# Index scores of a decoder trunk: the rectified scores of two neighbouring pieces in one tile, added by one VectorE operation

## The chip, the cores and the metric

One core of one Trainium2 chip runs the whole program. The metric is the device time of one execution in microseconds (us), and the time of the kernel before is the median of three runs. Times inside the program come from one profiled execution, counted from the start of its span. The engines are PE (TensorE), DVE (VectorE), ACT (ScalarE), POOL (GpSimd) and SP (SyncE, which issues most DMAs); each has its own queue and works it off in order.

## The reference

Two post-norm layers run over 2048 tokens of width 1024: forgetting attention, then sparse attention (DSA) with a light indexer. The change lies in the indexer of the second layer. For each token it computes eight heads of scores against all earlier tokens, rectifies them, weighs them by a number per token and head, sums over the heads, and keeps the 256 largest:

```python
isc = jnp.einsum('bqhd,bsd->bqhs', qi_b, ki).astype(jnp.float32) * di ** -0.5
isc = jnp.einsum('bqhs,bqh->bqs', jax.nn.relu(isc), wi_b)
isc = jnp.where(kpos[None, None, :] <= qpos[None, :, None], isc, -jnp.inf)
_, idx = lax.top_k(isc, k_sel)
```

The selected keys then go through an ordinary softmax attention, a SiLU gate and an output projection.

## The kernel before

The program runs in phases. After the first layer's attention and output projection comes the stage around the change: the projections of the second layer (`dsa_jobs`: `first`, `second`, `rest`), with the indexer's jobs woven in between them by `weave`. Then the second layer's attention and its output projection follow. The build uses a scheduler (`TCA`, "schedule_with_timeline_sim") that plays the program through with modelled times and so fixes the order of every engine's queue; the order of jobs in the source gives the priorities.

The index works on 14 query tiles of 128 tokens, tiles 2 to 15, in three groups (`GROUPS`): 7 to 2, 11 to 8, 15 to 12. Scores of query tile `qt` span n = (qt + 1) * 128 keys and stand in SBUF as one row of f32 per token (`x`, in the tiles GA, GB, GC: the first group in GA, the second in GB, the third in GC for tiles 15 and 14 and in GA again for 13 and 12). While one group is scored, the threshold search of the group before it runs (`step`, `move`, `finish`: counting passes on ACT, L1554, and on DVE, L1550, and chains of small operations on DVE).

`scores` (L1464) makes one query tile. It loads the queries `qs` (L1470, tag QS, two buffers), and for every head cuts the n keys into pieces of at most 512 columns (`cuts`, L1094): 1 piece for tiles 2 and 3, 2 for tiles 4 to 7, 3 for 8 to 11 (of which the last has 256 to 512 columns), 4 for 12 to 15. A piece is

- two matmuls (L1477, L1478) into a PSUM bank that `unit` gives out in a cycle of S, U, S, U, S (three banks S, two U),
- one ACT operation (L1480): scale and Relu from PSUM into an SBUF tile of tag SC (three buffers of 512 f32),
- one DVE operation: for head 0 a multiplication by the token's weight into `x` (L1483, TENSOR_SCALAR), for heads 1 to 7 a multiplication and addition onto `x` (L1485, SCALAR_TENSOR_TENSOR).

The projections of the same stage use the banks T and O, evacuated by ACT and DVE (L371, L378, L379) or, where a rotation is applied, by `rope` (L1247 to L1250); its table `kcs` is loaded into an SC buffer. Weights of a projection come from DRAM to RW (L353), are scaled and split by ACT and POOL (L341, L328, L325). Tag QS is a buffer of 1024 f32 and also serves, before this stage, a layer-norm row, and after it the first masks of the second attention (L964, read by L1054).

Each phase lays its tiles out in the order of `ORDER` with the sizes (in f16 elements) of `SIZE`; phase 6, the index, lies behind the eight KV tiles that hold the projections' input.

Of the kernel before, what the change touches and what calls it, by code (L numbers as in the profile page):

```python
# [15 lines left out]
F16 = mybir.dt.float16  # L16
OP = mybir.AluOpType
AF = mybir.ActivationFunctionType
# [29 lines left out]
BUFS = {"W": 6, "E": 8, "RW": 3, "QS": 2, "SC": 3, "ty": 9, "tz": 4, "tb": 2, "mb": 2}  # L48
PHASE = ({"KV": 8}, {"K": 4, "V": 2, "PT": 1, "PU": 1, "PX": 1, "PR": 4, "PP": 3, "I": 1, "N": 3},
         {"K": 4, "V": 2, "PT": 1, "PU": 1, "PX": 1, "PR": 4, "PP": 3, "M": 1, "N": 3}, {"P": 8},  # L50
         {"A": 3, "X": 15}, {"P": 8}, {})
ORDER = ((), ("N", "I", "PR", "PT", "pad1", "PU", "K", "PP", "V", "PX"),
         ("N", "M", "PX", "PR", "K", "V", "PP", "pad2", "PT", "PU"), ("pad3", "P"), ("A", "X"), (),
         ("st", "GB", "u", "GA", "GC", "spare"))
SIZE = {"K": 2048, "V": 4096, "PT": 8192, "PU": 8192, "PX": 8192, "PR": 4096, "PP": 4096, "I": 128, "N": 256,
        "M": 2432, "pad1": 3200, "pad2": 896, "pad3": 4096, "P": 4096, "A": 4096, "X": 4096, "st": 4096,
        "u": 3584, "spare": 4096, "GA": 8448, "GB": 10752, "GC": 7936}
TURNED = ("PT", "PU", "PX")

PS_BUFS = {"S": 3, "T": 2, "U": 2, "O": 1}  # L60
# [170 lines left out]
class Trunk:  # L231
# [1232 lines left out]
    def scores(self, qt, st, x):  # L1464
        nc = self.nc
        n = (qt + 1) * 128
        self.stack(n)
        qs = self.t("QS", [128, 8, 128], F16)
        ready = nc.gpsimd.memset(x[:, n - 1:n], 0.0)
        load = nc.sync.dma_start(qs, self.scr["qis"].rearrange("(h p) t -> p h t", p=128)  # L1470
                                 [:, :, qt * 128:(qt + 1) * 128])
        self.follow(load, ready, "no scores without a place for them")
        for h in range(H):
            for a, b in self.cuts(n):
                w = b - a
                ps = self.unit()
                nc.tensor.matmul(ps[:, :w], qs[:, h], st[:, 0, a:b], start=True, stop=False)  # L1477
                nc.tensor.matmul(ps[:, :w], qs[:, h], st[:, 1, a:b], start=False, stop=True)  # L1478
                t = self.t("SC", [128, w])
                nc.scalar.activation(t, ps[:, :w], AF.Relu, scale=self.scales[:, 24:25])  # L1480
                w1 = self.wi[:, qt, h:h + 1]
                if h == 0:
                    nc.vector.tensor_scalar(x[:, a:b], t, w1, None, op0=OP.mult)  # L1483
                else:
                    nc.vector.scalar_tensor_tensor(x[:, a:b], t, w1, x[:, a:b], op0=OP.mult, op1=OP.add)  # L1485

    def select(self, tiles, st):
        nc, V = self.nc, self.nc.vector
# [185 lines left out]
```

## Time and profile before

| | us |
|---|---|
| median of three runs (2772.9 to 2783.97) | 2780.16 |
| the profiled execution | 2781.16 |
| its span | 2779.4 |
| first and last start of the score additions (L1485) | 1451.2, 1862.0 |
| last projection matmul ahead of the second attention | 2055.17 |

The profile gives for each engine its busy time in any stretch, for each group of instructions the count, the mean duration and the idle time of its engine just ahead of them with what ended that idle time, and for each wait who waited for whom. "Busy" of PE overlaps from one matmul to the next. The granted clock is TensorE's, as a share of the full 2.4 GHz.

### The profile page before, as it was taken

Reading aid. Unit: us, or ns where it says so; the run is one execution under the profiler, and the core shown is the slowest. Engines: PE = TensorE matmul, PEld = TensorE weight load, DVE = VectorE, ACT = ScalarE, POOL = GpSimd, SP = SyncE. Lnnn points to the kernel's source line nnn. Section 1 sums busy time; section 2 is a strip of 40 time slices with the busy share of each in tenths; the row PEclk is TensorE's granted clock in tenths of the full one; section 3 lists DMA queues with packets and bytes.
Section 4 is the critical chain, followed back from the end, with each engine's and each line's share of the span. In section 5 each row is a group of like instructions: output and inputs, shape, how many; then the busy total and the mean of one; then the engine's idle time right before and its main releaser. Section 6 shows DMA issues by size and latency. Waiting matters only on the chain. (4 is left out here: it accounts for less than half of the span.)

```text
span 2779.4 us, 44011 instructions
## 1 busy us (share of the span) xinstructions
PE 2517.8 (91%) x15919; PEld 1636.5 (59%) x15919; DVE 1888.0 (68%) x4662; ACT 1419.7 (51%) x2283; POOL 858.8 (31%) x601
## 2 busy tenths in 40 slices
PE   8788989999988889889999989899978888888898
PEld 7688534444665666668845444444435666666687
DVE  4786655444766666667748899888955666666565
ACT  6464343322665666632326876774535666666310
POOL 3465643330333334442210211110013333333421
PEclk9899999999999999999999999999989999999999
DMA  7456645214988888864332432222678888777642
GB/s 263 162 187 204 211 126 173 76 65 151 210 204 171 184 188 181 165 198 141 124 97 61 123 90 64 69 75 82 197 217 190 192 178 184 173 163 151 183 144 88
DMA packets 583809, 424.20 MB, mean 153 GB/s; under 512 B 398048, under 2 KB 473584, under 8 KB 583584
## 3 DMA queue, kind: packets, MB, share of 16 engines
q1 hardware_dynamic: 580544, 412.78, 56.2%
q10 hardware_dynamic: 1984, 4.20, 0.5%
q0 software_dynamic: 1056, 4.36, 0.4%
q8 instruction: 125, 2.05, 0.3%
q14 instruction: 100, 0.82, 0.1%
HBM read 219.88 MB, written 109.08 MB: 118 GB/s over the span
## 5 line engine op out<-in xcount | busy, mean ns | idle before, releaser
L325 POOL TENSOR_TENSOR PP<-PR,PP 128x640 f16<-128x640 f32 (+3 forms) x192 | 375.8, 1971 | 697.0 <-ACT PP L1076 525.5
L1068 ACT ACTIVATE PR<-PR,ty,small 128x1152 f32<-128x1152 f32 (+15 forms) x256 | 330.1, 1290 | 249.5 <-DVE ty L1067 245.5
L325 POOL TENSOR_TENSOR W<-RW,W 128x512 fp32r<-128x512 f32 (+1 forms) x124 | 160.0, 1310 | 540.7 <-ACT W L328 469.5
L325 POOL TENSOR_TENSOR W<-A,W 128x512 f16<-128x512 f32 x114 | 136.5, 1218 | 228.8 <-ACT W L328 192.2
L320 PEld LDWEIGHTS <-W 128*128 128x128 f16 x1184 | 116.3, 98 | 147.1 <-issue 13.9
L321 PEld LDWEIGHTS <-W 128*128 128x128 f16 x1184 | 116.3, 98 | 137.9 <-issue 2.9
L319 PEld LDWEIGHTS <-W 128*128 128x128 f16 x1184 | 116.6, 98 | 137.3 <-issue 3.2
L1076 ACT ACTIVATE PP<-PR 128x640 f16<-128x640 f32 (+3 forms) x192 | 186.2, 980 | 18.0 <-DMA PX<-PP 7.5
L320 PEld LDWEIGHTS <-V 128*128 128x128 f16 x1152 | 117.0, 102 | 104.4 <-issue 81.8
L319 PE MATMUL T<-KV,W 128*128 128x512 f16 x464 | 176.9, 381 | 0.4 <-DVE E L1250 0.4
L320 PE MATMUL T<-KV,W 128*128 128x512 f16 x464 | 177.1, 382 | 0.0
L321 PE MATMUL T<-KV,W 128*128 128x512 f16 x464 | 176.9, 381 | 0.0
L328 ACT ACTIVATE W<-RW 128x512 fp32r<-128x512 f32 (+1 forms) x124 | 73.4, 629 | 181.6 <-PE U L320 93.6
L1054 DVE CUSTOM_DVE_ANT_0 PR<-S,W,ty 128x512 f32<-128x512 f32 (+3 forms) x209 | 138.8, 664 | 38.0 <-PE S L1049 18.1
L319 PEld LDWEIGHTS <-V 128*128 128x128 f16 x1152 | 116.9, 101 | 64.0 <-DMA PX<-PP 17.0
L319 PE MATMUL S<-K,E 128*128 128x512 f16 (+3 forms) x379 | 132.3, 349 | 11.5 <-DVE ty L1054 10.7
L378 ACT ACTIVATE SC<-E,tz 128x512 f16<-128x512 f32 (+1 forms) x78 | 50.8, 682 | 172.5 <-DVE E L540 102.6
L320 PE MATMUL S<-K,E 128*128 128x512 f16 (+3 forms) x379 | 132.3, 349 | 0.0
L321 PE MATMUL S<-K,E 128*128 128x512 f16 (+3 forms) x379 | 131.9, 348 | 0.0
L1480 ACT ACTIVATE SC<-S,small 128x512 f32<-128x512 f32 (+2 forms) x182 | 111.8, 635 | 35.4 <-DVE GC L1485 7.1
L321 PEld LDWEIGHTS <-V 128*128 128x128 f16 x1152 | 117.2, 102 | 20.1 <-issue 0.8
L1088 PE MATMUL T<-ident,PR 128*128 128x128 f32 x768 | 116.6, 277 | 3.4 <-DVE PU L325 1.7
(503 smaller groups left out, 7836.0 us busy)
## 6 DMA issues: line engine op xcount, KB each, us to landing
A<-in_fw SPq DMA_DIRECT2D x38, 512.0 KB
QS<-in_fw SPq DMA_DIRECT2D x32, 512.0 KB
E<-scr_g SPq DMA_DIRECT2D x64, 256.0 KB
scr_og<-SC SPq DMA_DIRECT2D x64, 256.0 KB
RW<-scr_og SPq DMA_DIRECT2D x64, 256.0 KB
E<-scr_q SPq DMA_DIRECT2D x62, 256.0 KB
V<-scr_v SPq DMA_DIRECT2D x28, 512.0 KB
scr_g<-E SPq DMA_DIRECT2D x48, 256.0 KB
```

What stands on the lines that cost most here:

```text
L319: first = mm(o, lh, rh, start=start, stop=False, skip_group_check=True)
L320: mm(o, lh, rl, start=False, stop=False, skip_group_check=True)
L321: mm(o, ll, rh, start=False, stop=stop, skip_group_check=True)
L325: eng.tensor_tensor(out=o, in0=a, in1=b, op=OP.subtract)
L328: self.nc.scalar.activation(hi, src, AF.Copy)
L378: nc.scalar.activation(out[0], src, AF.Copy, scale=scale)
L1054: nc.vector.tensor_tensor_reduce(out=row[:, lo:hi], in0=sc[:, lo - a:hi - a], in1=bias, op0=OP.add, op1=OP.min, scale=-1.0, scalar=3e38 if ...
L1068: nc.scalar.activation(row, row, AF.Exp, bias=up, scale=neg, accum_out=cs["l"][:, j:j + 1])
L1076: nc.scalar.activation(hi, row, AF.Copy)
L1088: nc.tensor.transpose(ps[:, (k - a) * 128:(k - a + 1) * 128], row[:, k * 128:(k + 1) * 128], self.ident)
L1480: nc.scalar.activation(t, ps[:, :w], AF.Relu, scale=self.scales[:, 24:25])
```

## The change

The queries move to a tag of their own, `qs`, with two buffers at the end of phase 6. The score pieces move from SC to QS: two neighbouring pieces of one head, or the single last one, are rectified by their ACT operations into one QS tile side by side, and one DVE operation multiplies, or multiplies and adds, over both, up to 1024 columns. Matmuls, ACT operations, PSUM banks and loads keep their number and size.

```diff
-         {"A": 3, "X": 15}, {"P": 8}, {})
+         {"A": 3, "X": 15}, {"P": 8}, {"qs": 2})
...
-         ("st", "GB", "u", "GA", "GC", "spare"))
+         ("st", "GB", "u", "GA", "GC", "spare", "qs"))
...
-        "u": 3584, "spare": 4096, "GA": 8448, "GB": 10752, "GC": 7936}
+        "u": 3584, "qs": 1024, "spare": 4096, "GA": 8448, "GB": 10752, "GC": 7936}
...
-        qs = self.t("QS", [128, 8, 128], F16)
+        qs = self.t("qs", [128, 8, 128], F16)
...
         for h in range(H):
-            for a, b in self.cuts(n):
-                w = b - a
-                ps = self.unit()
-                nc.tensor.matmul(ps[:, :w], qs[:, h], st[:, 0, a:b], start=True, stop=False)
-                nc.tensor.matmul(ps[:, :w], qs[:, h], st[:, 1, a:b], start=False, stop=True)
-                t = self.t("SC", [128, w])
-                nc.scalar.activation(t, ps[:, :w], AF.Relu, scale=self.scales[:, 24:25])
+            cuts = self.cuts(n)
+            for i in range(0, len(cuts), 2):
+                two = cuts[i:i + 2]
+                lo, hi = two[0][0], two[-1][1]
+                t = self.t("QS", [128, hi - lo])
+                for a, b in two:
+                    ps = self.unit()[:, :b - a]
+                    nc.tensor.matmul(ps, qs[:, h], st[:, 0, a:b], start=True, stop=False)
+                    nc.tensor.matmul(ps, qs[:, h], st[:, 1, a:b], start=False, stop=True)
+                    nc.scalar.activation(t[:, a - lo:b - lo], ps, AF.Relu, scale=self.scales[:, 24:25])
                 w1 = self.wi[:, qt, h:h + 1]
                 if h == 0:
-                    nc.vector.tensor_scalar(x[:, a:b], t, w1, None, op0=OP.mult)
+                    nc.vector.tensor_scalar(x[:, lo:hi], t, w1, None, op0=OP.mult)
                 else:
-                    nc.vector.scalar_tensor_tensor(x[:, a:b], t, w1, x[:, a:b], op0=OP.mult, op1=OP.add)
+                    nc.vector.scalar_tensor_tensor(x[:, lo:hi], t, w1, x[:, lo:hi], op0=OP.mult, op1=OP.add)
```

## Rows read from the trace of the kernel before

**Rows 1.** The page, part 1: busy time of each engine, its share of the span and its instructions.

```profile
PE 2517.8 (91%) x15919; PEld 1636.5 (59%) x15919; DVE 1888.0 (68%) x4662; ACT 1419.7 (51%) x2283; POOL 858.8 (31%) x601
```

**Rows 2.** Busy time by stretch: the stretch and its length; busy time (and instructions) of PE, PE's weight loads, DVE, ACT and POOL; PE's granted clock; the share of the DMA engines and GB/s.

```profile
1448.00:1533.00 85.00, 83.04 (x428) 42.22 (x426) 66.57 (x132) 56.89 (x104) 7.08 (x6) 1.00 0.22 59
1533.00:1600.00 67.00, 62.78 (x288) 29.29 (x288) 59.01 (x167) 55.96 (x107) 15.87 (x13) 0.95 0.43 124
1600.00:1863.00 263.00, 238.63 (x1111) 108.97 (x1109) 244.96 (x768) 197.63 (x357) 36.48 (x34) 0.99 0.28 75
1863.00:2055.00 192.00, 188.38 (x866) 84.83 (x865) 163.46 (x375) 93.59 (x136) 10.97 (x14) 0.99 0.46 149
...
1533.00:1545.00 12.00, 7.78 (x23) 3.07 (x23) 10.37 (x24) 9.33 (x16) 1.97 (x2) 0.72 0.32 92
```

**Rows 3.** PE's waits from 1448 to 1863 us (who waited, for whom: us in total, times, longest), and below them the same wait of L1477 from 1600 to 1863 us alone (us, times).

```profile
PE S L1477 <- ACT SC L1480: 19.0, 19, 3.1
PE U L1477 <- ACT SC L1480: 9.8, 10, 2.9
...
  ACT SC L1480: 24.2, 24
```

**Rows 4.** ACT's waits from 1600 to 1863 us.

```profile
ACT RW L341 <- DMA RW<-in_dw: 14.8, 8, 3.8
ACT SC L1480 <- DVE GC L1485: 9.9, 5, 3.8
ACT SC L1480 <- DVE GB L1485: 9.7, 10, 1.9
...
ACT SC L1480 <- DVE GA L1485: 4.6, 7, 1.8
```

**Rows 5.** The chain that ended last, where the projections end: start, length, what.

```profile
2037.25 0.22 PE O L319
2055.17 0.23 PE O L321
```

**Rows 6.** The instructions of L1480 and of L1485: engine, operation, out<-in, count, duration in ns as least, median and most, first and last start, and their shapes.

```profile
L1480 ACT ACTIVATE SC<-S,small x182: 461/678/757, 1449.9 to 1860.2; 128x512 f32<-128x512 f32 x118, 128x384 f32<-128x384 f32 x35, 128x256 f32<-128x256 f32 x29
L1480 ACT ACTIVATE SC<-U,small x122: 454/682/742, 1449.3 to 1858.0; 128x512 f32<-128x512 f32 x82, 128x384 f32<-128x384 f32 x21, 128x256 f32<-128x256 f32 x19
...
L1485 DVE SCALAR_TENSOR_TENSOR GA<-SC,flog,GA x126: 466/740/1717, 1451.2 to 1862.0; 128x512 f32<-128x512 f32 x70, 128x384 f32<-128x384 f32 x28, 128x256 f32<-128x256 f32 x28
L1485 DVE SCALAR_TENSOR_TENSOR GB<-SC,flog,GB x84: 474/744/1724, 1538.9 to 1688.1; 128x512 f32<-128x512 f32 x56, 128x384 f32<-128x384 f32 x14, 128x256 f32<-128x256 f32 x14
...
L1485 DVE SCALAR_TENSOR_TENSOR GC<-SC,flog,GC x56: 569/737/1350, 1694.7 to 1781.0; 128x512 f32<-128x512 f32 x49, 128x384 f32<-128x384 f32 x7
```

**Rows 7.** Prices of DVE operations. First two of the timeline (start, length, count at the end, idle time ahead), then groups by shape from 1448 to 1863 us (busy us, mean ns of one, idle ahead).

```profile
1455.27 3.40 DVE L1485 SCALAR_TENSOR_TENSOR GA<-SC,flog,GA 128x512 f32<-128x512 f32 x5 [2.02 <-ACT SC L1480]
...
1466.06 0.75 DVE L1485 SCALAR_TENSOR_TENSOR GA<-SC,flog,GA 128x512 f32<-128x512 f32 x1 [0.92 <-ACT SC L1480]
...
L1609 DVE SCALAR_TENSOR_TENSOR spare<-GA,sv,small 128x1024 bf16<-128x1024 f32 x1 | 1.3, 1283 | 0.0
...
L1483 DVE TENSOR_SCALAR GA<-SC,flog 128x512 f32<-128x512 f32 x10 | 4.7, 479 | 0.7 <-ACT SC L1480 0.7
...
L1483 DVE TENSOR_SCALAR GA<-SC,flog 128x256 f32<-128x256 f32 x4 | 1.4, 346 | 0.0
```

**Rows 8.** The instructions of L1485 from 1600 to 1863 us, columns as in rows 6; those of GC stand there.

```profile
L1485 DVE SCALAR_TENSOR_TENSOR GB<-SC,flog,GB x56: 474/739/1656, 1601.4 to 1688.1; 128x512 f32<-128x512 f32 x30, 128x256 f32<-128x256 f32 x14, 128x384 f32<-128x384 f32 x12
...
L1485 DVE SCALAR_TENSOR_TENSOR GA<-SC,flog,GA x56: 466/741/752, 1788.5 to 1862.0; 128x512 f32<-128x512 f32 x35, 128x256 f32<-128x256 f32 x14, 128x384 f32<-128x384 f32 x7
```

**Rows 9.** Three small operations of the search on DVE, from the timeline. The second doesn't read what the first wrote; the third reads what the second wrote.

```profile
1924.63 0.16 DVE L1574 SCALAR_TENSOR_TENSOR sv<-sv 128x4 f32<-128x4 f32 x1
1924.71 0.16 DVE L1575 SCALAR_TENSOR_TENSOR sv<-sv 128x4 f32<-128x4 f32 x1
1924.90 0.17 DVE L1503 TENSOR_TENSOR sv<-sv 128x8 f32<-128x8 f32 x1
```

**Rows 10.** The timeline around 1535 us; in brackets the idle time ahead and what ended it.

```profile
1534.29 0.74 DVE L1247 SCALAR_TENSOR_TENSOR SC<-O,small,SC 64x512 f32<-64x512 f32 x1
...
1536.41 0.69 ACT L1480 ACTIVATE SC<-U,small 128x512 f32<-128x512 f32 x1 [2.12 <-DVE GB L1483]
...
1537.15 0.40 PE L1477 MATMUL U<-st,QS 128*128 128x512 f16 x1 [2.93 <-ACT SC L1480]
```

**Rows 11.** Three rows of SP's timeline, and the first reads of a mask in QS (L1054, as in rows 6).

```profile
1816.86 1.28 SPq L964 DMA_DIRECT2D QS<-scr_mask  x3
...
1848.52 1.46 SPq L353 DMA_DIRECT2D RW<-in_dw  x2
...
1856.64 2.33 SPq L964 DMA_DIRECT2D QS<-scr_mask  x2
...
L1054 DVE CUSTOM_DVE_ANT_0 PR<-U,QS x2: 672/677/682, 2049.3 to 2059.2; 128x512 f32<-128x512 f32 x2
```

**Rows 12.** A wait of ACT for weights, and PE's wait behind it, from their timelines.

```profile
1786.52 1.35 ACT L341 ACTIVATE RW<-RW,small 128x512 f32<-128x512 f32 x2 [3.77 <-DMA RW<-in_dw]
...
1788.49 0.38 PE L1477 MATMUL S<-st,QS 128*128 128x512 f16 x1 [3.07 <-ACT SC L1480]
```

## The prediction

> **What bounds the kernel now.** I read the page's busy shares first [rows 1]: PE is busy for 91% of the span, DVE for 68%, so nothing of DVE is worth time unless it holds PE up somewhere. The edited lines run between 1448 and 1863 us, so next comes the table of stretches [rows 2]. It shows three regimes. From 1448 to 1533 PE is busy for 83.0 of 85 us and DVE idles for 18 us: PE bounds. From 1533 to 1600 one stretch of 12 us stands out: PE 7.8 of 12 us busy, granted clock 0.72. From 1600 to 1863 the roles are mixed: DVE is busy for 245.0 of 263 us and PE for 238.6, so PE loses 24.4 us. From 1863 on PE is full again (188.4 of 192).
>
> The waits say what PE lacked. In the whole stage nearly all of it is one row pair: matmuls of L1477 that wait for a PSUM bank, which ScalarE (L1480) has not emptied yet: 19.0 + 9.8 us, of which 24.2 us lie between 1600 and 1863 [rows 3]. ScalarE in turn waited there for VectorE's score operations, 9.9 + 9.7 + 4.6 us, because no place was free for the rectified piece, and apart from that 14.8 us for weights from DRAM [rows 4]. So the chain is DVE (L1485) -> SC place -> ACT -> PSUM -> PE. After it PE works to 2055 us, where the last projection leaves and attention begins [rows 5]. What PE gains between 1448 and 1863 moves that point, and everything behind it, one for one.
>
> **The change part by part.**
>
> *Merged operations.* The stage has 182 + 122 = 304 pieces, so 304 ACT operations, 126 + 84 + 56 = 266 additions (L1485), and therefore 38 multiplications (L1483) [rows 6]. By `cuts`, query tiles 2 and 3 have one piece per head, 4 to 7 two, 8 to 11 three, 12 to 15 four. Pairing saves 1 operation per head for tiles 4 to 11 and 2 for tiles 12 to 15: 16 per head, 128 in all; 176 DVE operations are left. ACT and PE keep all theirs.
>
> The price of a merge: five additions of 512 columns in a row take 3.40 us, one alone 0.75, so each further one costs (3.40 - 0.75)/4 = 0.66 us; there is an overlap of 0.09 us with its neighbour. The kernel before has no addition of 1024 columns with these tiles, but the same operation on 1024 columns takes 1.283 us at L1609 [rows 7]; less the same overlap that is 1.19. A merge thus saves 2 x 0.66 - 1.19 = 0.13 us of DVE time. Upper bound: without any overlap 2 x 0.744 (the median in [rows 6]) - 1.28 = 0.21; the multiplications give the same (2 x 0.346 - 0.479 = 0.21, [rows 7]). Lower bound: none, since it is the count of starts that falls; a saving below zero would need a 1024-column operation above 1.33 us, which no row shows. I take 0.13, because DVE runs back to back where it matters.
> The Trainium skill ("Perfetto Trace Analysis", Optimizing Scalar/DVE Operations) puts VectorE's overhead per instruction on SBUF at about 60 ns and says that grouping into larger operations improves throughput if the engine is saturated. By that figure the sum below would be 64 x 0.06 = 3.8 us and the time an estimated 2776; the rows show about twice the figure.
>
> *Where it counts.* The 32 merges of tiles 4 to 7 fall before 1533, where DVE idles for 18 us: nothing. Should that cover be gone, they would be worth 4 us. The third group (15, 14) and the first buffer's second use (13, 12) lie wholly between 1600 and 1863 [rows 6, 8]: 64 merges, 64 x 0.13 = 8.3 us. Of the second group (11 to 8, tile GB) 56 of 84 additions lie there [rows 8], so 32 x 56/84 = 21 merges or 2.8 us; I count none of it, because of the next part.
>
> *Places.* Three SC places of 512 columns become two QS places of up to 1024. Tiles 12 to 15 need two pairs per head: each place takes a pair, the lead grows from three pieces to four. Tiles 4 to 7 the same. Tiles 8 to 11 need a pair and a single piece, so the pairs always fall into one place and the singles into the other. ACT can then refill the pair's place only after VectorE has read it. Back to back, a head took 2 x 0.66 + 0.5 = 1.9 us on DVE; now fill (2 x 0.68, the median of L1480 in [rows 6], about 1.3 with the overlap of two in a row) and read (1.2) come one after the other: 2.5 us. That is up to 0.65 us per head for 32 heads, 21 us, if nothing stands between the heads on DVE. These 32 heads are spread over 150 us, 4.7 us each, with other work of DVE between them, so most of it should be covered. I set it against the 2.8 us above and keep 21 us as the bound of the range.
>
> *Repeated sums.* With one operation per head in tiles 4 to 7, an addition reads what the one directly ahead of it wrote. Small operations of the search start 0.08 us apart when the second doesn't need the first, and 0.19 when it does [rows 9]. 32 x 0.11 = 4 us, all before 1533, hidden by DVE's idle 18 us; 4 us if not.
>
> *Places shared no longer.* SC is left to the `kcs` table and others. Around 1534 the table held one of three SC places while VectorE was turning it; ACT waited 2.12 us, PE 2.93 us, and the clock fell to 0.72 [rows 2, 10]. Now three score pieces' worth of room stays. That stretch of 12 us lost 4.2 us of PE and 12 x 0.28 = 3.4 us of clock: 0 to 7.6 us, of which I take 0, since DVE itself was busy for most of it.
>
> *Queues.* The loads of `qs` have the same count, size and number of places (two), only another address, behind `spare`, where no tile lay before in this phase: 0. The loads of attention's masks go to QS places as well: three at 1817 us, two at 1857 [rows 11]. They now need VectorE to have read the scores, so they come at 1862 at the earliest, 190 us ahead of their first reader at 2049 [rows 11]: 0. But if the planner leaves the first of them in SP's queue at 1817, the weight loads at 1848 stand behind it for up to 14 us. ACT's waits for such loads already put PE back by 3.07 us at 1788 [rows 12]; a repeat would cost about that.
>
> **The sum.** The profiled execution took 2781.2 us (span 2779.4), 1.0 above the median of 2780.2; the change is a difference, so it is taken from the median: 2780.2 - 8.3 = 2772 us.
>
> **The rivals.**
> (1) *All of the score waits go.* PE's 24.2 us between 1600 and 1863, less what began as a late weight load (3.07 at 1788, [rows 12], and perhaps as much again), and the 7.6 us around 1534: 18 + 8 = 26 us, 2754. For it: ACT's waits on score operations sum to 24 us [rows 4], and a backlog shrinks faster than the load. Against: DVE stays over 90% busy there.
> (2) *The waits are a matter of order.* The queues are ordered by a planner that plays the program through; what PE meets is a mismatch of its times with the real ones, and DVE's 8 us become idle time between search steps. 2780.
> (3) *The single place of the pairs decides.* Tiles 8 to 11 run at 2.5 instead of 1.9 us per head, from 1535 to 1688; it decides as soon as VectorE has less than 0.65 us of other work between two heads, and PE's lead of five PSUM banks (two matmuls of 0.22 us each, [rows 5], so 2.2 us) is used up, as it was at each of the waits in [rows 3]. 32 x 0.65 = 21 us, 2801; the same with half of it, 2790. For it: the group's additions are among those that ACT waits for most [rows 4]. Against: 4.7 us per head.
> The rule of the Trainium skill that speaks for this one stands in the same section of "Perfetto Trace Analysis": where VectorE isn't saturated but causes bubbles on other engines, "breaking up instructions may allow work to be completed sooner". By that rule, the trace agrees that DVE's score operations cause PE's bubbles; with 93% busy it is near saturation, so both halves of the section apply in part.
> (4) *It doesn't do what it says*: the wide operation costs as much as two. the operation at L1609 speaks against it; 2780, told with (2).
>
> **How the numbers follow.** A measurement of this kernel can tell about 0.5% from no change: 13.9 us. Forecast, a gain of 4 to 14 us: 0.33. Rival (1) and all gains above 14 us: 0.30. Rivals (2) and (4), within 4 us: 0.12. A part of (3), a loss of 4 to 14 us: 0.05. Rival (3) in full: 0.20. So faster by over 0.5%: 0.30; within 0.5%: 0.33 + 0.12 + 0.05 = 0.50; slower: 0.20. The range runs from a little below rival (1) to half-way and a bit into rival (3): 2750 to 2796.
>
> **What would show it.** Right: 176 operations on L1483 and L1485, wide ones at about 1.28 us; busy DVE time of L1483 and L1485 down by some 27 us; PE's wait for L1480 between 1600 and 1863 down from 24 to about 16 us; PE's last projection some 8 us earlier than 2055. Wrong: ACT waiting longer for the second group's places (GB) than the 9.7 us of before, or PE's waits moving to other lines; mask loads with SP waiting behind them for tens of us. The forecast fails if DVE's saved time reappears as idle time while PE's waits stay.

## The result

| | before | after |
|---|---|---|
| median of nine runs, us | 2775.59 (2770.25 to 2789.67) | 2760.94 (2755.95 to 2767.12) |
| the profiled execution / its span, us | 2781.16 / 2779.4 | 2759.65 / 2757.9 |
| after / before | | 0.9945, 95% interval 0.9929 to 0.9961 |

The change saves 14.65 us of 2775.59. The interval in microseconds (worked out: 0.0039 and 0.0071 of 2775.59) is 11 to 20 us. The forecast was 8.3 us less; its 2772 us starts from the median of three runs, 2780.16.

In the changed file every line from the loop of `scores` on stands three or four lines further down: matmuls L1481 and L1482, Relu L1483, multiplication L1486, addition L1488.

**Where the time went.** The two profiled executions differ by 21.5 us of span, more than the medians do. To see which part belongs to the change I cut both at two points that exist in every version: the start of the last transposition (L1211) of the first layer's result, and the evacuation (L371) of the last projection, where the second attention begins. Before ran from 1395.7 to 2055.5, after from 1385.9 to 2030.1 us. So 9.8 us arose ahead of the first cut, where both programs hold the same instructions in the same order on PE (thirteen profiles put that point between 1385.1 and 1399.0 us). The stage between the cuts fell from 659.8 to 644.2, by 15.6 us. What follows the second cut grew by 3.9 us (723.9 to 727.8). Stage and rest are therefore told apart below. A stage or a rest from one profile is itself unsure by several microseconds: from the second cut on, before, after, `qs_alone`, `b_p96` and `a_p96` (below) have the same order on PE and on VectorE, and their rests are 723.9, 727.8, 723.9, 728.6 and 718.8 us.

The whole stage of before by busy time (columns as in rows 2):

```profile
1395.70:2055.50 659.80, 625.63 (x2939) 289.92 (x2938) 551.26 (x1465) 413.52 (x718) 75.02 (x70) 0.99 0.35 101
```

The same of after, and its parts, which answer to [rows 2]:

```profile
1385.90:2030.10 644.20, 619.49 (x2938) 288.55 (x2937) 527.83 (x1337) 414.40 (x717) 77.05 (x70) 0.99 0.35 104
...
1448.00:1533.00 85.00, 85.00 (x446) 44.20 (x445) 65.59 (x116) 59.73 (x109) 13.33 (x10) 1.00 0.30 82
1533.00:1600.00 67.00, 62.86 (x289) 28.53 (x288) 56.17 (x168) 56.42 (x111) 17.15 (x13) 0.97 0.38 115
1600.00:1852.00 252.00, 233.21 (x1096) 107.30 (x1095) 225.62 (x671) 195.16 (x352) 32.07 (x30) 0.99 0.26 68
1533.00:1545.00 12.00, 12.00 (x57) 5.48 (x56) 6.82 (x30) 11.94 (x24) 3.42 (x3) 1.00 0.56 173
1590.00:1600.00 10.00, 6.47 (x24) 2.56 (x23) 8.30 (x21) 4.40 (x9) 2.30 (x1) 0.83 0.27 89
```

VectorE is busy for 23.4 us less in the stage (551.26 to 527.83), with 128 instructions fewer. PE has the same work (2938 matmuls): its busy time fell by 6.1 us and its idle time by 9.5 us (659.80 - 625.63 = 34.2; 644.20 - 619.49 = 24.7). Most of the busy time goes with the clock: before's stage has 17 us at the lower level of 1.2 GHz, after's has 7. The 12 us from 1533, which had 7.78 us of work at clock 0.72 [rows 2], are now full at 1.00 (the twelve from 1523.2, the same place counted from the first cut, are so too); another dip, at 1590, is new.

VectorE's score operations of after, grouped (busy us, mean ns of one | idle time ahead), first with all shapes, then the full ones alone:

```profile
L1488 DVE SCALAR_TENSOR_TENSOR GA<-QS,flog,GA 128x1024 f32<-128x1024 f32 (+5 forms) x70 | 71.9, 1029 | 23.5 <-ACT QS L1483 22.1
L1488 DVE SCALAR_TENSOR_TENSOR GB<-QS,flog,GB 128x1024 f32<-128x1024 f32 (+4 forms) x56 | 52.9, 950 | 3.9 <-ACT QS L1483 3.7
L1488 DVE SCALAR_TENSOR_TENSOR GC<-QS,flog,GC 128x1024 f32<-128x1024 f32 (+1 forms) x28 | 35.7, 1274 | 5.6 <-ACT QS L1483 5.6
L1486 DVE TENSOR_SCALAR GA<-QS,flog 128x1024 f32<-128x1024 f32 (+5 forms) x10 | 7.0, 705 | 0.4 <-ACT QS L1483 0.4
L1486 DVE TENSOR_SCALAR GB<-QS,flog 128x1024 f32<-128x1024 f32 (+4 forms) x8 | 4.4, 565 | 0.1
L1486 DVE TENSOR_SCALAR GC<-QS,flog 128x1024 f32<-128x1024 f32 (+1 forms) x4 | 2.8, 716 | 0.0
...
L1488 DVE SCALAR_TENSOR_TENSOR GA<-QS,flog,GA 128x1024 f32<-128x1024 f32 x21 | 26.9, 1281 | 11.6 <-ACT QS L1483 11.3
```

The counts add up to 176. The busy times add up to 174.7 us; the 304 operations of before add up to 200.8 in the same view (its additions follow; its multiplications have 16.5 us), so 26.1 us are gone. One wide addition takes 1.28 us.

```profile
L1485 DVE SCALAR_TENSOR_TENSOR GA<-SC,flog,GA 128x512 f32<-128x512 f32 (+1 forms) x126 | 82.7, 681 | 18.2 <-ACT SC L1480 17.0
L1485 DVE SCALAR_TENSOR_TENSOR GB<-SC,flog,GB 128x512 f32<-128x512 f32 (+2 forms) x84 | 61.2, 741 | 7.1 <-ACT SC L1480 6.7
L1485 DVE SCALAR_TENSOR_TENSOR GC<-SC,flog,GC 128x512 f32<-128x512 f32 (+1 forms) x56 | 40.4, 735 | 3.1 <-ACT SC L1480 3.0
```

PE's waits for the Relu in the stage of after (us in total, times, longest), and below them the wait of L1481 from 1600 to 1852 us alone, which answer to [rows 3]:

```profile
PE S L1481 <- ACT QS L1483: 14.9, 13, 3.5
PE U L1481 <- ACT QS L1483: 7.5, 6, 2.0
...
  ACT QS L1483: 18.5, 17
```

ACT's waits from 1600 to 1852 us, which answer to [rows 4]:

```profile
ACT RW L341 <- DMA RW<-in_dw: 16.0, 9, 3.0
ACT QS L1483 <- DVE GB L1488: 7.3, 7, 1.8
ACT QS L1483 <- DVE GA L1488: 4.4, 2, 2.2
ACT QS L1483 <- DVE GC L1488: 3.1, 3, 1.9
```

The chain that ended last, at the end of the projections, which answers to [rows 5]:

```profile
2029.89 0.23 PE O L321
```

PE's waits for the Relu fell from 28.8 to 22.4 us in the stage, ACT's on score additions between 1600 and the end of the scores from 24.2 to 14.8 us. ACT's wait for weights stayed. The last projection leaves 25.3 us earlier, 9.8 of which were there ahead of the change's code.

### The profile page after: what moved, and what is told of

Its sections match the earlier page's. It is cut to its first block, busy times and chain, and to the rows that moved or that the text cites. A ratio compares the mean times of both kernels' runs of the same rounds, so it can differ in the third digit from the quotient of the medians.

```text
span 2757.9 us, 43730 instructions
## 1 busy us (share of the span) xinstructions
PE 2514.1 (91%) x15919; PEld 1636.3 (59%) x15919; DVE 1857.4 (67%) x4534; ACT 1420.3 (51%) x2283; POOL 861.6 (31%) x601
## 5 line engine op out<-in xcount | busy, mean ns | idle before, releaser
L325 POOL TENSOR_TENSOR PP<-PR,PP 128x640 f16<-128x640 f32 (+3 forms) x192 | 375.6, 1970 | 703.3 <-ACT PP L1076 551.7
L325 POOL TENSOR_TENSOR W<-RW,W 128x512 fp32r<-128x512 f32 (+1 forms) x124 | 162.2, 1328 | 525.1 <-ACT W L328 468.3
L325 POOL TENSOR_TENSOR W<-A,W 128x512 f16<-128x512 f32 x114 | 136.4, 1216 | 221.2 <-ACT W L328 221.2
L321 PEld LDWEIGHTS <-W 128*128 128x128 f16 x1184 | 116.0, 98 | 137.3 <-issue 1.0
L1076 ACT ACTIVATE PP<-PR 128x640 f16<-128x640 f32 (+3 forms) x192 | 186.2, 980 | 18.2 <-DMA PX<-PP 7.2
L1054 DVE CUSTOM_DVE_ANT_0 PR<-S,W,ty 128x512 f32<-128x512 f32 (+3 forms) x209 | 138.8, 664 | 41.4 <-PE S L1049 20.8
L319 PE MATMUL S<-K,E 128*128 128x512 f16 (+3 forms) x379 | 132.8, 351 | 11.5 <-DVE ty L1054 10.7
L321 PEld LDWEIGHTS <-V 128*128 128x128 f16 x1152 | 118.0, 102 | 20.8 <-issue 0.8
L1483 ACT ACTIVATE QS<-S,small 128x512 f32<-128x512 f32 (+2 forms) x182 | 112.1, 635 | 35.2 <-DVE GB L1488 10.2
```

What stands on the lines that cost most here:

```text
L319: first = mm(o, lh, rh, start=start, stop=False, skip_group_check=True)
L321: mm(o, ll, rh, start=False, stop=stop, skip_group_check=True)
L325: eng.tensor_tensor(out=o, in0=a, in1=b, op=OP.subtract)
L1054: nc.vector.tensor_tensor_reduce(out=row[:, lo:hi], in0=sc[:, lo - a:hi - a], in1=bias, op0=OP.add, op1=OP.min, scale=-1.0, scalar=3e38 if ...
L1076: nc.scalar.activation(hi, row, AF.Copy)
L1483: nc.scalar.activation(t[:, a - lo:b - lo], ps, AF.Relu, scale=self.scales[:, 24:25])
```

## The experiments

**Theory A**: time is gained because VectorE spends less time per score, so that places and PSUM banks come free earlier. **Theory B**: it is the room, since the scores have places of their own and a longer lead, and the width of the operation matters little. **Theory C**: the planner puts the queues into another order when anything is edited, and the gain is an accident of that order. A smaller question beside them is rival (3), the single place of the pairs of tiles 8 to 11.

This table has all programs but narrow. Stage, VectorE's busy time in it, and rest (from the stage's end to the end of the span) come from one profile each; "waits" are PE's waits for the Relu of the scores in the stage, both banks, and the ratio is that of the whole time to the kernel before on the same chip.

| | operations | stage | DVE busy | waits | rest | ratio (95%) |
|---|---|---|---|---|---|---|
| before | 304 | 659.8 | 551.3 | 28.8 | 723.9 | 1 |
| after | 176 | 644.2 | 527.8 | 22.4 | 727.8 | 0.9945 (0.9929 to 0.9961) |
| split | 304 | 656.5 | 551.9 | 25.5 | 739.4 | 1.0022 (1.0006 to 1.0038) |
| qs_alone | 304 | 660.5 | 551.3 | 27.2 | 723.9 | 1.0011 (0.9994 to 1.0028) |
| five | 304 | 654.5 | 549.5 | 20.8 | 728.0 | 0.998 (0.9964 to 0.9996) |
| m12 | 240 | 657.6 | 545.5 | 28.0 | 729.0 | 0.9993 (0.9974 to 1.0013) |
| m8 | 272 | 664.6 | 550.6 | 32.9 | 724.6 | 0.9995 (0.9976 to 1.0014) |
| single_sc | 176 | 656.3 | 535.4 | 27.5 | 727.7 | 0.999 (0.9972 to 1.0007) |
| pad | 304 | 654.0 | 547.0 | 23.9 | 725.3 | 0.9963 (0.9946 to 0.998) |
| b_p96 | 304 | 656.5 | 548.9 | 25.1 | 728.6 | 0.9996 (0.9981 to 1.0011) |
| a_p96 | 176 | 650.9 | 534.0 | 23.0 | 718.8 | 0.9975 (0.9959 to 0.9992) |
| b_p04 | 304 | 659.5 | 553.5 | 28.5 | 723.2 | 1.0026 (1.0006 to 1.0045) |
| a_p04 | 176 | 645.0 | 531.9 | 21.5 | 723.2 | 0.9971 (0.9951 to 0.9991) |

**split**: the changed kernel with its places and its order of jobs, but one VectorE operation per piece again.

```diff
-                if h == 0:
-                    nc.vector.tensor_scalar(x[:, lo:hi], t, w1, None, op0=OP.mult)
-                else:
-                    nc.vector.scalar_tensor_tensor(x[:, lo:hi], t, w1, x[:, lo:hi], op0=OP.mult, op1=OP.add)
+                for a, b in two:
+                    if h == 0:
+                        nc.vector.tensor_scalar(x[:, a:b], t[:, a - lo:b - lo], w1, None, op0=OP.mult)
+                    else:
+                        nc.vector.scalar_tensor_tensor(x[:, a:b], t[:, a - lo:b - lo], w1, x[:, a:b], op0=OP.mult, op1=OP.add)
```

> The changed kernel with its places as they are (pairs side by side in QS, the queries in a tag of their own), but one VectorE operation for each piece again, 304 instead of 176. Theory A, that the time of the merged operations is what counts: the gain goes, the ratio to the kernel before is 0.997 to 1.003, and ScalarE's and TensorE's waits in the stage are those of before. Theory B, that the room counts (four pieces instead of three, SC no longer shared with the rotation table): the ratio stays at 0.993 to 0.996. Theory C, that any edit shifts the planned order and so the waits: no particular value, 0.992 to 1.006, with no relation to VectorE's busy time.

The stage of split (columns as in rows 2):

```profile
1386.20:2042.70 656.50, 622.13 (x2938) 288.66 (x2937) 551.87 (x1459) 414.11 (x717) 71.96 (x67) 0.99 0.34 99
```

VectorE's busy time is back at that of before, and 12.3 of the 15.6 us of the stage with it: for A, against B. The whole time says the same more surely: the ratio of split and that of the change lie far apart (1.0006 to 1.0038, 0.9929 to 0.9961). But the whole program is slower than before although its stage is 3.3 us shorter: its rest is 15.5 us longer, with unchanged code there. The order of the queues in it did change, so this can be a sign of C, which would move time in the attention too; a part of the 15.5 us is this one execution, since by the medians split is only 6.5 us slower than before (2780.47 and 2773.93).

**qs_alone**: before, with the queries in a tag of their own and nothing else.

```diff
+         {"A": 3, "X": 15}, {"P": 8}, {"qs": 2})
...
+        "u": 3584, "qs": 1024, "spare": 4096, "GA": 8448, "GB": 10752, "GC": 7936}
...
-        qs = self.t("QS", [128, 8, 128], F16)
+        qs = self.t("qs", [128, 8, 128], F16)
```

> The kernel before with one part of the change alone: the queries have their own tag behind the other tiles of the phase; scores stay in three SC places, one VectorE operation a piece, and QS lies empty in this stage. Theories A and B: nothing moves, 0.997 to 1.003, TensorE's waits for L1480 stay near 29 us. Theory C: it may move by up to 0.6% to either side without any change of VectorE's work; if it does, part of the change's 0.55% is not to be put down to VectorE.

Nothing changed: the order of the queues of PE, DVE and ACT is that of before, instruction by instruction, the stage takes 660.5 us and VectorE 551.3. Because the order is the same, the two stages differ by the execution alone, by 0.7 us. That is one pair; the rests named in the first section, also of one order, spread by 9.8 us.

**five**: before, with the queries moved as in qs_alone and the pieces, unmerged, in five places by turns (three SC, two QS).

```diff
-                t = self.t("SC", [128, w])
+                self.place = (getattr(self, "place", -1) + 1) % 5
+                t = self.t("QS" if self.place in (1, 3) else "SC", [128, w])
```

> The kernel before with the queries in their own tag and the score pieces in five places by turns, three of SC and two of QS, each a single piece, one VectorE operation a piece. Theory A: 0.997 to 1.003, since VectorE's time is as before. Theory B: the same gain as the change or more, 0.990 to 0.996, and ScalarE's waits for VectorE's score operations (24 us between 1600 and 1863 us in the kernel before) fall by half.

Room alone brings 5.3 us of the stage, and 5 us of the whole (0.998), about a third of the gain. PE waits less for the Relu than in the changed kernel (20.8 against 22.4 us), yet the stage is 10.3 us longer: PE also waits 4.1 us once for the load of the queries and 5.0 us for evacuations of the projections (L379, 1.3 us in after). B explains at most this part; by the spread between single profiles, even that isn't certain.

**narrow**: before, but the additions leave out the first 128 columns of every second piece.

```diff
-                    nc.vector.scalar_tensor_tensor(x[:, a:b], t, w1, x[:, a:b], op0=OP.mult, op1=OP.add)
+                    o = 128 if i % 2 else 0
+                    nc.vector.scalar_tensor_tensor(x[:, a + o:b], t[:, o:], w1, x[:, a + o:b], op0=OP.mult, op1=OP.add)
```

> The kernel before, places and number of operations unchanged, but the additions of heads 1 to 7 leave out the first 128 columns of every second piece, so that part of the sum is missing: 112 additions are 128 columns shorter, 0.133 us each by the 1.04 ns a column of the profile (744 ns for 512, 1804 for 1536 columns), 14.9 us of VectorE's time, about what the 128 merges save (128 x 0.13 = 17 us). Theory A: the same gain as the change, 0.993 to 0.997. Theory B: 0.997 to 1.003.

It took 4039.54 us, ratio 1.4558 (1.4527 to 1.4589). Two groups of narrow, from 1380 to 3400 us, show why:

```profile
L1600 DVE MAX8 tz<-GA 128x8 f32<-128x1024 f32 (+7 forms) x256 | 295.3, 1153 | 0.0
L1603 DVE MATCH_REPLACE8 GA<-tz,GA 128x1024 f32<-128x1024 f32 (+7 forms) x256 | 292.7, 1143 | 0.0
```

In the kernel before these run 8 times each on GA. The sums left out let the threshold search end elsewhere, a branch of the program that depends on the data (31 more rounds of taking the largest eight) was entered for every group. With the same operations on GB and GC that is 1263 us more of VectorE's time, and the program took 1266 us longer. The run says nothing about A, B or C.

**m12** and **m8**: the change for some tiles alone, in both cases with the queries moved; other tiles keep single pieces in SC. In m12 the tiles 12 to 15 are paired (64 merges), in m8 the tiles 8 to 11 (32 merges).

```diff
-            for a, b in self.cuts(n):
...
+            cuts = self.cuts(n)
+            step = 2 if qt >= 12 else 1
+            for i in range(0, len(cuts), step):
+                two = cuts[i:i + step]
...
+                t = self.t("QS" if step == 2 else "SC", [128, hi - lo])
```

(In m8 the condition is `8 <= qt < 12`.)

> Pairs in QS and one operation for both only in query tiles 12 to 15 (64 of the 128 merges); the other tiles rectify single pieces into SC as before. The stage is measured from the last transpose of the first output projection (L1211) to the last gate operation (L371): 659.8 us in the kernel before, 644.2 in the changed one, 723.9 and 727.8 us behind it. Theory A (the time of merged operations counts, where VectorE is the bound): 64 x 0.13 = 8.3 us off the stage, 651 us or less. Theory D, the gain comes from the second group (tiles 8 to 11) or from the 12 us around 1535: the stage stays at 657 to 660 us. What lies behind the stage may move by up to 15 us with the planned order.

> Pairs only in query tiles 8 to 11 (32 of the 128 merges), the lone third pieces and all other tiles in SC. Theory A by the prediction: 21 of these merges lie where VectorE bounds, 2.8 us off the stage, 657 us. Theory D: more than half of the 15.6 us, 652 us or less. Rival (3) of the prediction doesn't apply, since pairs have both places.

The stage of m8, and its longest wait of PE:

```profile
1389.00:2053.60 664.60, 625.72 (x2939) 289.94 (x2937) 550.58 (x1433) 414.16 (x718) 75.99 (x70) 0.98 0.35 100
```

```profile
PE S L1482 <- ACT SC L1484: 16.5, 9, 6.4
```

m12 gave 2.2 us of its stage, m8 lost 4.8. Neither measures what its merges are worth, because the order moved as well: in m8 VectorE's score operations have 6.5 us less busy time than before (194.3 against 200.8, summed over the groups of a view), but its search operations, the same 962, have 3.9 us more (304.1 against 300.2; the last section shows beside what), and its stage is the longest of all. So which tiles carry the gain stays open.

**single_sc**: the changed kernel, with pieces that have no partner in SC. That gives the pairs of tiles 8 to 11 both QS places.

```diff
-                t = self.t("QS", [128, hi - lo])
+                t = self.t("QS" if len(two) == 2 else "SC", [128, hi - lo])
```

> The changed kernel, but a lone piece (tiles 2 and 3, and the third piece of tiles 8 to 11) is rectified into SC, so that the pairs of tiles 8 to 11 take both QS places by turns. If pairs that always fall into one place cost time (rival 3 in part), the stage falls below 644.2 us, by up to 6 us, and ScalarE's waits for GB, 12.4 us in the changed kernel, fall. If not, it stays within 2 us of 644.2.

ACT's waits for additions onto GC and GB in the stage of single_sc:

```profile
ACT QS L1483 <- DVE GC L1488: 10.3, 5, 3.6
...
ACT QS L1483 <- DVE GB L1488: 2.4, 1, 2.4
```

The second group's wait is gone (12.4 us over the stage of after, 2.4 here), as the hand-over of rival (3) wants it. It brought nothing: the wait of the third group rose from 3.1 to 10.3 us and the stage to 656.3 us, with all 128 merges in place. Rival (3)'s place in the queue is real, but removing it doesn't help. And a program with all merges can lose most of the gain, to its order or to the single pieces that lie in SC again: in the 12 us from 137.3 us behind the first cut, the place of the stall at 1535 in before, PE is busy for 9.55 us here and for 12.00 in after.

**pad**: the changed kernel with one extra VectorE operation of 64 columns behind each paired operation. It multiplies the start of the piece by one after it was read. Head 0 has one as well, so there are 128, not the 112 of the expectation.

```diff
+                if len(two) == 2:
+                    nc.vector.tensor_scalar(t[:, :64], t[:, :64], 1.0, None, op0=OP.mult)
```

> The changed kernel with one more VectorE operation behind each paired addition: the first 64 columns of the rectified pair times 1, in place, which nothing reads; 112 of them, about 0.1 to 0.15 us each by the small operations of the profile, 11 to 17 us of VectorE's time given back; places, pairs and loads stay. Theory A: 60 of these 112 in the stretch that VectorE bounds, so 6 to 9 us of the stage's gain go, and with the clock up to 15: 650 to 659 us. If the number of hand-overs between ScalarE and VectorE counts and not VectorE's time, it stays at 643 to 647 us.

The stage of pad, and ACT's wait for the extra operations in it:

```profile
1392.80:2046.80 654.00, 625.15 (x2939) 289.64 (x2938) 547.01 (x1461) 413.32 (x718) 77.09 (x69) 0.99 0.34 100
```

```profile
ACT QS L1483 <- DVE QS L1490: 43.2, 20, 6.4
```

The number of VectorE's score operations is 304 again. Its busy time rises by 19.2 us (0.15 us for each of the 128), and the stage by 9.8 us: again half a microsecond of stage per microsecond of VectorE. For A, but less surely than split. Of the 9.8 us, 5.7 are PE's busy time (619.49 to 625.15 for the same work) and 4.1 its idle time. The extra operation also holds the place longer (ACT waits 43.2 us for it), so a part may belong to that. And by the whole time the loss isn't clear of noise: the intervals of pad (0.9946 to 0.998) and of the change (0.9929 to 0.9961) overlap.

**b_p96, a_p96, b_p04, a_p04**: to size C, before and after were each built in two more orders. The index jobs are woven into the projections of `second` over a stretch from 0 to 1 of it; here to 0.96, or from 0.04. Nothing else is edited.

```diff
-PREW = (0.0, 1.0)
+PREW = (0.0, 0.96)
```

(In the p04 pair it is `(0.04, 1.0)`; b_ is before with this edit, a_ is after with it.)

> The kernel before with the weaving of the first ten index jobs drawn 4% earlier over the projections beside them (PREW ends at 0.96 in place of 1.0): the same instructions, another planned order from there on. Theory A (the merges' VectorE time makes the gain): the stage from L1211 to L371 stays near 660 us here and near 644 us in the pair's other half. Theory C (the planned order makes a large part of it): this one lies anywhere from 650 to 666 us.

> The changed kernel with the same shift (PREW ends at 0.96). Theory A: the stage is 642 to 647 us, 13 to 17 us below the kernel before with the same shift. Theory C: it falls back to 650 to 658 us, and the difference to its partner is 3 to 9 us, what 64 to 128 merges of 0.07 to 0.13 us can give.

> The kernel before with the first ten index jobs woven in from 4% on (PREW begins at 0.04 in place of 0): the same instructions, another order. Theory A: the stage stays near 660 us. Theory C: anywhere from 650 to 666 us.

> The changed kernel with PREW from 0.04. Theory A: the stage is 642 to 647 us, 13 to 17 us below its partner. Theory C: 650 to 658 us, 3 to 9 us below its partner. Taken over the three pairs, A says that the mean difference is about 15 us, C that it is 5 to 10 us and that the first pair is the farthest out.

The stages of the four, in this order:

```profile
1391.20:2047.70 656.50, 624.55 (x2939) 289.39 (x2938) 548.94 (x1465) 415.16 (x717) 73.94 (x70) 0.99 0.35 101
1399.00:2049.90 650.90, 621.24 (x2939) 288.36 (x2937) 533.96 (x1337) 414.42 (x718) 79.22 (x70) 0.99 0.35 103
1392.20:2051.70 659.50, 627.02 (x2942) 290.34 (x2941) 553.50 (x1465) 413.71 (x717) 74.94 (x70) 0.98 0.34 100
1385.10:2030.10 645.00, 619.38 (x2938) 288.70 (x2937) 531.86 (x1334) 413.08 (x718) 78.98 (x70) 0.99 0.36 104
```

With equal edits the change shortens the stage by 15.6 us (as given), 5.6 (p96) and 14.5 us (p04): a mean of 11.9. The p96 pair came out as C had said, the p04 pair as A had, and the mean lies between the 15 of A and the 5 to 10 of C. The medians of the whole time differ by 14.65, 5.5 (2773.07 to 2767.59) and 18.2 us (2780.43 to 2762.24). Three of three are gains, so the gain is no accident of one order, though that of p96 alone isn't clear of noise (0.9981 to 1.0011 and 0.9959 to 0.9992 overlap); a single order puts it anywhere from 5 to 18 us. The rest has means of 725.2 us without and 723.3 with the change, so nothing is given back there as a rule.

A line through the thirteen stage times over VectorE's busy time (worked out from the table) has a slope of 0.55 us per us, a correlation of 0.84, and leaves 3.4 us of scatter. The scatter holds order and execution together, and VectorE's busy time holds what its operations lose beside POOL (last section), so the slope is no price of VectorE's own work. How much is A and how much C can't be read closer here.

## Why the prediction was right or wrong

**What bounds the kernel**: right. PE's waits at the end of the path VectorE, place, ACT, PSUM, PE fell by 6.4 us, of 9.5 us that PE idled less in the stage. When VectorE's time came back in split and pad, most of the stage came back.

**Price of a merge**: right. Two wide additions of after with what follows each (start, length):

```profile
1698.46 1.28 DVE L1488 SCALAR_TENSOR_TENSOR GC<-QS,flog,GC 128x1024 f32<-128x1024 f32 x1
1699.65 0.22 DVE L1603 TENSOR_SCALAR tz<-small,sv 128x8 f32<-128x8 f32 x1
...
1706.02 1.28 DVE L1488 SCALAR_TENSOR_TENSOR GC<-QS,flog,GC 128x1024 f32<-128x1024 f32 x1
1707.22 0.22 DVE L1603 TENSOR_SCALAR tz<-small,sv 128x8 f32<-128x8 f32 x1
```

The next operation starts 1.19 or 1.20 us after the wide one, as put together from [rows 7]; so 0.13 us are saved per merge. The summed busy time fell by 26.1 us where 27 were named; 4.1 of these come from fewer meetings with POOL (last section). The Trainium skill ("Perfetto Trace Analysis", Optimizing Scalar/DVE Operations) puts the overhead at about 60 ns; these rows give twice that. The time worked out from its figure was an estimated 2776 us, a gain of 3.8 us; 14.65 were measured.

**The terms that were mis-sized.** The sum took 64 of 128 merges, 8.3 us, and put the rest at nothing. The stage gave 15.6 us in this order and 11.9 as a mean of three orders. One term that was put at nothing did give something, as the runs show: the places shared no longer (below), at 0 of 0 to 7.6 us. For the other two, "hidden by DVE's idle 18 us" for the merges of tiles 4 to 7 and "set against" the hand-over for those of tiles 8 to 11, it stays open: all 128 merges would be 16.6 us, and m12 and m8 couldn't tell which count. PE idled 9.5 us less in the stage, and 6.1 us of its busy time came on top. A term that the sum didn't have is what VectorE's operations lose beside POOL: 7.6 us less in this order (last section).

**Places**: the cost was rightly left out of the sum. GB's wait of ACT did rise over the stage, from 10.7 to 12.4 us, but fell between 1600 and the scores' end, from 9.7 [rows 4] to 7.3. One new stall is there, in the timeline of after:

```profile
1591.59 0.75 DVE L1247 SCALAR_TENSOR_TENSOR E<-T,small,E 128x512 f32<-128x512 f32 x1 [2.96 <-DMA E<-in_qs]
...
1593.05 1.28 DVE L1488 SCALAR_TENSOR_TENSOR GB<-QS,flog,GB 128x1024 f32<-128x1024 f32 x1
...
1594.42 1.26 ACT L1483 ACTIVATE QS<-S,small 128x512 f32<-128x512 f32 x2 [4.13 <-DVE GB L1488]
...
1595.16 0.32 PE L1481 MATMUL S<-st,qs 128*128 128x384 f16 x1 [3.53 <-ACT QS L1483]
```

Read it from the top: VectorE waits 2.96 us for a load into E, the wide addition stands behind that in its queue, the place stays full, ACT waits 4.13 us, PE 3.53, and its clock is 0.83 over these 10 us. The chain begins with the load. That a second place for the pairs would have kept ACT from waiting behind it was not tried by itself.

**Places shared no longer**: I took 0 of 0 to 7.6 us, and this term was too small. The 12 us of the stall lie 137.3 us behind the first cut in before. At that place, split and `b_p96` have:

```profile
1523.50:1535.50 12.00, 12.00 (x60) 5.69 (x58) 7.40 (x25) 10.24 (x20) 3.42 (x3) 1.00 0.48 143
1528.50:1540.50 12.00, 7.99 (x24) 3.18 (x24) 10.38 (x24) 9.33 (x17) 1.94 (x2) 0.72 0.33 94
```

Every program whose early tiles keep all their pieces in SC beside the table (before, qs_alone, m12, m8, b_p96, b_p04) has 7.8 to 8.3 us of PE there, at clock 0.72. In after, split, pad, a_p96 and a_p04, where no piece lies in SC, PE is busy for 12.00 of 12 us at 1.00. So it goes with the places and not with the merges, of which split has none: some 4 us of PE's idle time, and the clock. In after the stall at 1590 took the gain away again (across the 67 us from 1533 PE is busy 62.86 us, before 62.78), so that zero came out there was luck. Five, with pieces in both, has 11.32 of 12 us at 0.86, and a shorter stage by 5.3 us.

**Queues**: no cost, as said. SP's rows of after:

```profile
1849.44 1.27 SPq L964 DMA_DIRECT2D QS<-scr_mask  x3
...
1851.29 0.90 SPq L964 DMA_DIRECT2D QS<-scr_mask  x2
1852.68 0.33 SPq L353 DMA_DIRECT2D RW<-in_dw  x1
```

The planner put the mask loads at 1849 us, where the places had just come free, and the weights behind them left 0.5 us later. They didn't stay at 1817 [rows 11].

**PE's waits and the end of the projections**: the wait between 1600 and the end of the scores fell from 24.2 to 18.5 us (about 16 was named), the last projection came 15.6 us earlier by the stage (8 was named).

**The rivals.** (1), 26 us by the end of all score waits, didn't happen: 22.4 of 28.8 us are left. But its stretch at 1534 did go. (2), no gain but a matter of planned order, didn't happen, since all three pairs gain; but order does move the time: by the medians the kernel before is 8 us slower in the order of b_p04 than as given (2780.43 and 2772.22). The stages of single profiles differ by 3 to 6 us between orders, and how much of that is the execution wasn't separated. (3) fell with single_sc. (4) fell with the price. The largest chance, 0.50, was on a change within 0.5%. The measured 0.55% lies just beyond that bound, in what was given 0.30, and its interval (0.39 to 0.71%) on both sides. The direction and the path were right; the gain was 1.8 times the forecast.

What share of the 14.65 us is VectorE's time, what is room and what is this order, is not settled to better than the 5 us or more by which orders and executions differ.

## What to carry to other kernels

- A sum of the terms that are sure is a lower part of a forecast. Here it came out at half of what the stage gave, and a range of 0 to 7.6 us that was taken as 0 held a gain in all three orders of the change. Where a range has only gains in it, carry its middle into the sum.
- Where a planner fixes the order of the queues, most edits deal a new order (of those here only qs_alone kept it on PE, VectorE and ACT); build before and after in two or three neighbouring orders and compare the pairs, or a few microseconds of order are taken for the effect of the change. Stages read from one profile each need repeats, too.
- Put a removed cost back in its pure form rather than taking the change apart by tiles: splitting the operation in the same places gave a clear answer by the whole time, the tiles gave none.

## What was not expected of the hardware

A wide addition that reads what the one directly ahead wrote starts later. In tile 7 of after there is one addition per head, onto the same 1024 columns:

```profile
1445.47 4.06 DVE L1488 SCALAR_TENSOR_TENSOR GA<-QS,flog,GA 128x1024 f32<-128x1024 f32 x3 [2.23 <-ACT QS L1483]
...
1456.27 1.28 DVE L1488 SCALAR_TENSOR_TENSOR GA<-QS,flog,GA 128x1024 f32<-128x1024 f32 x1 [2.08 <-ACT QS L1483]
```

Each further one takes (4.06 - 1.28)/2 = 1.39 us instead of 1.19. The prediction had 0.11 us for this from small operations; it is 0.20. Ahead of such an addition VectorE's queue holds a semaphore wait (42 of them at L1488, 21 ns each, one for each of the seven additions in the six tiles 2 to 7), and the addition starts 0.10 us after the end of the one before it; the operations of L1603 above, on other data, start 0.08 us or 0.09 us before that end.

VectorE's busy time holds more than its own work. In after:

```profile
1596.53 1.28 DVE L1488 SCALAR_TENSOR_TENSOR GB<-QS,flog,GB 128x1024 f32<-128x1024 f32 x1
1596.54 2.30 POOL L325 TENSOR_TENSOR E<-E,E 128x512 f16<-128x512 f32 x1 [7.94 <-DMA E<-in_qc]
...
1597.73 1.14 DVE L1570 TENSOR_SCALAR sv<-sv 128x3 f32<-128x3 f32 x1
...
1598.79 0.15 DVE L1571 TENSOR_SCALAR sv<-sv 128x3 f32<-128x3 f32 x1
```

The small operation at 1597.73 takes 1.14 us, the next one 0.15, and the long one ends with POOL's operation (1598.87 and 1598.84). In the stage of after, 25 operations of VectorE take over 0.3 us longer than the median of the same operation with the same shapes, 19.9 us together (worked out from the trace), and every one of them overlaps an operation of POOL at L325, though only 9% of VectorE's operations do. In before there are 35 with 27.5 us, in split 39 with 34.5, in pad 31 with 27.4. With the change it is less in all three orders: 19.9, 24.6 and 23.4 us against 27.5, 28.5 and 30.8.

So of the 23.4 us by which VectorE's busy time fell, 7.6 are time not lost beside POOL, and of the 24.0 that came back in split 14.6. The same 962 operations of the threshold search kept VectorE busy for 294.6 us in after and 304.1 in m8 (summed over their groups); 15.4 and 22.7 of these are such losses. A saving counted in busy time is blurred by that much from one order to the next. Why the two hold each other up, and whether fewer operations meet POOL less often as a rule, no run here shows.
